# Six plain contraction tiles instead of two in each down projection, and the table of relative positions made in the mixer

## The chip, the cores and the metric

The kernel runs on one core of one Trainium2 chip. The metric is the device time of one execution in microseconds (us). TensorE (PE) multiplies, VectorE (DVE), ScalarE (ACT) and GpSimd (POOL) work on tiles in on-chip memory, and two engines issue the DMAs: SP the plain loads and stores, POOL those that add to their destination.

## The reference

A decoder layer on 512 tokens of width 1024, in float32: a half-step feed-forward block, a mixer of two kinds of attention, attention into a memory, a second feed-forward block; each is added to the residual stream and normalised. The parts that matter here:

```python
def swiglu(x, w1, w3, w2):
    return (jax.nn.silu(x @ w1) * (x @ w3)) @ w2          # D_FF = 2816 = 22 tiles of 128

h = layer_norm(ALPHA * h + 0.5 * swiglu(h, ffn1_w1, ffn1_w3, ffn1_w2), ln1_g, ln1_b)
mix = parallel_mixer(h, rel_bias, ...)                    # bias = rel_bias[t5_bucket(q_pos, k_pos)]
h = layer_norm(ALPHA * h + mix, ln2_g, ln2_b)
h = layer_norm(ALPHA * h + memory_attention(h, mem, ...), ln3_g, ln3_b)
h = layer_norm(ALPHA * h + 0.5 * swiglu(h, ffn2_w1, ffn2_w3, ffn2_w2), ln4_g, ln4_b)
```

`parallel_mixer` also needs one number `lam`, made from four short vectors by `exp(sum(q1*k1)) - exp(sum(q2*k2)) + lam_init`.

## The kernel before

Every float32 operand is split into a high and a low part (`split`: a cast, and a subtraction for the rest), and every product is three matmuls: high by high, high by low, low by high. A weight tile so split is called `..._hl`.

**Feed-forward block** (`ffn`, run as block 1 and block 4). The 22 contraction tiles f of the down projection are the 22 row tiles of the up projection. Tiles 0 and 1 of the up projection are plain. Tiles 2 to 21 come in ten pairs p1 to p10: `seven(p)` makes the 2x2 blocks of weights and tokens (or sums of them) meet in seven products instead of eight, each of 24 matmuls of 128x256, named `px`, `pz`, `py`, with weight blocks `wp_b` and their splits `wp_hl`. The down projection does the same for groups of four contraction tiles: `down7(g)` has seven products of 12 matmuls of 128x512, `dx`, `dy`, `dz`, with weights `wd_b`, `wd_hl` and token forms `A`. The loop runs p1, p2, group 0, p3, p4, group 1, and so on: two up pairs, one down group, five times. Groups 0 to 3 copy each product to a tile `st` (ScalarE) and POOL's DMA adds it into `acc` in DRAM. Within the last group the four token tiles of `acc` are loaded back into `res.acc` (`load_acc`, eight loads by SP, which must wait for the adding DMAs), and group 4's products are added into them by VectorE, 14 adds. At last `res.add` takes contraction tiles 20 and 21 as plain products (`res_w`, 48 matmuls of 128x512 for four token tiles and two halves of the columns), adds them and normalises token tile by token tile (`Norm`: `nmu`, `u`, `sq`, `ms`, `rs` on POOL, then `acc`). After blocks 1 to 3, TensorE transposes each normalised tile (`trh`, 8 transposes a tile), since the next stage wants it transposed in `hT`.

**Tables.** A generator `tables` waits until the planner's clock stands at 200 us; then it loads the constants, makes the table of relative positions (`bias_table`: load of `hot`, two small matmuls `rel`, a copy to `rows`, a store to `bias_dram`) and the number `lam` (`lam_calc`: load, product, sum, Exp). This falls into p7 of block 1.

**Mixer.** After block 1 come the first four gate tiles (`pw_gm`), the latents (`cq` and `ckv` for four token tiles each, transposed as `trc`), and the attention heads: `qr`, `vm`, `qn`, `kn` are a head's projections, `sm` its scores, `e` the exponentials, `trp_m` their transposes, `om` the weighed values; further gate tiles `pgm` are filler in between.

**Order.** Nothing is placed by hand. `Issue` is a planner in the program: generators yield work, TensorE's matmuls are issued as they come, each advancing the planner's clock by an estimate, and the other engines' operations wait in a list and are issued when their estimated start is due. So one generator that yields elsewhere can change the order of unrelated instructions near it. Each engine then works strictly in the order issued. There are three raw weight buffers (`wraw`), five split ones (`wsplit`), 20 general slots (`slot`) and eight PSUM banks.

Of the kernel before, what the change touches and what calls it, by code (L numbers as in the profile page):

```python
# [10 lines left out]
F32 = mybir.dt.float32  # L11
# [183 lines left out]
def layer(ctx: ExitStack, tc: tile.TileContext, a: dict, out: bass.AP):  # L195
# [421 lines left out]
    def plan_ffn(n, w1, w3, w2):  # L617
# [18 lines left out]
        for f in (20, 21):  # L636
            W.plan(f"w2_{n}_{f}", w2[f * P:(f + 1) * P])

    def ffn(n, src, ready=None):
        res = Residual(n, src)  # L640
        gT, sums, raw = {}, {}, {}
# [24 lines left out]
        def seven(p, late=()):  # L666
# [3 lines left out]
            def out(c, half, ps, sign):  # L670
# [3 lines left out]
                if half and p == 10:  # L674
# [46 lines left out]

        def down7(g, forms):
# [9 lines left out]
            def add(pss, h, c, sign, new=False):  # L732
                if g == 4:
                    for t in range(2):
                        dst = res.acc[2 * h + t][:, c * 512:c * 512 + 512]
                        dve.tensor_tensor(dst, dst, pss[t], op=ALU.add if sign > 0 else ALU.subtract)
                elif g == 0 and new:
# [4 lines left out]
                else:  # L742
                    st = slot(f"st{n}_{g}_{h}_{c}", F32)
                    for t in range(2):
                        act.activation(st[:, t], pss[t], AF.Copy, scale=sign)
                    pool.dma_start(rows(acc[h, c]), st, accum_op=ALU.add)
# [51 lines left out]
        for g in range(5):  # L798
            yield from seven(2 * g + 1)
            forms = Forms(g)  # L800
            late = {3: lambda: forms.make(1), 2: lambda: forms.make(2), 4: lambda: forms.make(5)}
            if g == 4:
                late[1] = load_acc
            yield from seven(2 * g + 2, late)
            yield from down7(g, forms)
        yield from res.add(lambda i, t: hl_of(gT[20 + i], slice(t * P, (t + 1) * P)), [f"w2_{n}_{f}" for f in (20, 21)], False, True)
# [4 lines left out]
    def bias_table():  # L811
# [4 lines left out]
        sp.dma_start(hot, a["onehot"])  # L816
        rows = arena.tile([8, REL], F32, tag="slot", name="rows")
# [5 lines left out]
        sp.dma_start(bias_dram.rearrange("h (p m) -> h p m", p=32), rows.unsqueeze(1).broadcast_to([8, 32, REL]))  # L823

# [4 lines left out]
    def lam_calc():  # L829
        room = slot("lam", F32, [P, 1024])  # L830
# [328 lines left out]
    def mixer():  # L1159
# [28 lines left out]
        ready = [h_ready[1, t] for t in range(NT)]  # L1188
        early = yield from project_halves([f"w_gm{j}" for j in range(EARLY)], ready)
# [219 lines left out]
    def tables():  # L1409
        mark = Mark()  # L1410
        mark.floor = 200000.0
        yield mark
        consts()
        bias_table()
        lam_calc()
# [100 lines left out]
```

## Time and profile before

| | |
|---|---|
| median of 3 runs | 1260.99 us (1260.83 to 1263.0) |
| profiled execution, its own time | 1261.45 us |
| its span | 1259.7 us |
| mean granted clock of TensorE | 0.988 |
| TensorE busy | 1214.5 us, 96%, 7530 matmuls |
| VectorE busy | 1019.4 us, 81%, 1590 instructions |
| ScalarE busy | 551.0 us, 44% |
| GpSimd busy | 105.5 us, 8% |

The times in the rows below are counted from the start of the span. A clock of 1.00 is 2.4 GHz, one of 0.50 is 1.2 GHz. A share of busy time says nothing of one stage; the rows are therefore cut to stages. In a timeline, "[4.41 <-DMA hot]" means that the engine stood idle 4.41 us just before and that the landing of `hot` ended it.

### The profile page before, as it was taken

To read this page: it belongs to the slowest core of one execution; us is meant where nothing else is said; L and a number is where in the kernel's file an instruction comes from. 1 tells how busy PE (TensorE), PEld (TensorE's weight loads), DVE (VectorE), ACT (ScalarE), POOL (GpSimd) and SP (SyncE) were. 2 spreads that over 40 slices of the span, in tenths; PEclk is the share of its full clock that TensorE was granted. 3 is DMA by queue.
4 is the path that set the end of the run, shared out by engine and by line. 5 is a ranking of instruction groups with operands and counts; after the bars stand their busy time and mean duration, and the time that the engine had idled before them with its cause. 6 is when DMAs were issued, how large, how long until landed. Compare 5 with 4: busy or idle time off the path is not lost. (4 is left out here: it accounts for less than half of the span.)

```text
span 1259.7 us, 19354 instructions
## 1 busy us (share of the span) xinstructions
PE 1214.5 (96%) x7530; PEld 1080.1 (86%) x7530; DVE 1019.4 (81%) x1590; ACT 551.0 (44%) x970; POOL 105.5 (8%) x101
## 2 busy tenths in 40 slices
PE   7999998999979999999999999999999999999995
PEld 5989897889869987877778889888899898999994
DVE  8999989789981799666665695555799999999998
ACT  5343635254432477434441244342453445445451
POOL 0001111111010000000000000000010102130300
PEclk9999999899979999999999999999999999999998
DMA  9749596869231321242233436244493667795941
GB/s 328 220 130 270 114 255 140 201 131 287 73 134 55 124 65 34 64 138 84 84 101 100 150 137 214 72 129 151 162 295 97 173 195 185 184 236 140 254 140 67
DMA packets 86591, 192.52 MB, mean 153 GB/s; under 512 B 7875, under 2 KB 9667, under 8 KB 86500
## 3 DMA queue, kind: packets, MB, share of 16 engines
q1 hardware_dynamic: 68004, 155.64, 37.1%
q0 software_dynamic: 18496, 35.66, 16.1%
q8 instruction: 59, 0.97, 0.3%
q14 instruction: 32, 0.26, 0.1%
HBM read 152.86 MB, written 38.40 MB: 152 GB/s over the span
## 5 line engine op out<-in xcount | busy, mean ns | idle before, releaser
L178 DVE TENSOR_TENSOR wp_hl<-wp_b,wp_hl 128x1024 fp32r<-128x1024 f32 x140 | 168.2, 1220 | 12.9 <-ACT wp_hl L178 10.6
L260 PE MATMUL pzwp<-S,wp_hl 128*128 128x256 f32 x960 | 124.2, 286 | 0.3 <-DVE S L178 0.3
L260 PE MATMUL pxwp<-S,wp_hl 128*128 128x256 f32 x960 | 122.6, 283 | 1.6 <-ACT p_wp L178 1.6
L260 PEld LDWEIGHTS pzwp<-S,wp_hl 128*128 128x128 f32 x960 | 120.0, 194 | 1.6 <-issue 1.1
L260 PE MATMUL pxwp<-hT,wp_hl 128*128 128x256 f32 x960 | 119.9, 281 | 1.3 <-ACT wp_hl L178 1.3
L260 PEld LDWEIGHTS pxwp<-hT,wp_hl 128*128 128x128 f32 x960 | 117.3, 188 | 4.2 <-ACT wp_hl L178 1.7
L260 PEld LDWEIGHTS pxwp<-S,wp_hl 128*128 128x128 f32 x960 | 118.3, 191 | 2.0 <-ACT p_wp L178 2.0
L178 ACT CAST wp_hl<-wp_b 128x1024 fp32r<-128x1024 f32 x75 | 78.7, 1051 | 93.3 <-PE pxwp L260 51.6
L260 PE MATMUL dx<-wd_hl,A 128*128 128x512 f32 x480 | 117.4, 391 | 1.6 <-DVE acc L178 1.2
L260 PEld LDWEIGHTS dx<-wd_hl,A 128*128 128x128 f32 x480 | 88.2, 188 | 21.2 <-issue 3.2
L178 DVE TENSOR_TENSOR wp_b<-wp_b,wp_b 128x1024 f32<-128x1024 f32 x80 | 97.4, 1219 | 0.6
L178 DVE TENSOR_TENSOR wd_hl<-wd_b,wd_hl 128x1024 fp32r<-128x1024 f32 x70 | 85.2, 1220 | 9.2 <-ACT wd_hl L178 9.2
L170 POOL DMA_DIRECT2D acc<-st x48 | 59.5, 1561 | 379.7 <-ACT st L178 205.1
L178 ACT CAST wd_hl<-wd_b 128x1024 fp32r<-128x1024 f32 x52 | 54.5, 1052 | 54.5 <-PE pxwp L260 24.9
L260 PE MATMUL pywp<-hT,wp_hl 128*128 128x256 f32 x480 | 60.6, 280 | 0.3 <-ACT wp_hl L178 0.3
L260 PE MATMUL dz<-wd_hl,A 128*128 128x512 f32 x240 | 59.2, 392 | 0.5 <-ACT st L178 0.3
L260 PEld LDWEIGHTS pywp<-hT,wp_hl 128*128 128x128 f32 x480 | 58.3, 188 | 0.5 <-ACT wp_hl L178 0.5
L260 PE MATMUL pw<-hT,w_hl 128*128 128x256 f32 (+1 forms) x288 | 49.8, 333 | 6.8 <-DVE w_hl L178 5.0
L260 PEld LDWEIGHTS dz<-wd_hl,A 128*128 128x128 f32 x240 | 44.5, 188 | 11.0 <-ACT st L178 1.1
L260 PEld LDWEIGHTS pw<-hT,w_hl 128*128 128x128 f32 x288 | 42.2, 194 | 13.5 <-ACT hT L178 7.2
L178 DVE CAST wp_hl<-wp_b 128x1024 fp32r<-128x1024 f32 x65 | 46.1, 710 | 7.4 <-PE pzwp L260 6.1
L260 PE MATMUL pgd<-hT,w_gd_hl 128*128 128x512 f32 x192 | 47.5, 400 | 0.0
(333 smaller groups left out, 2300.9 us busy)
## 6 DMA issues: line engine op xcount, KB each, us to landing
wp_b<-in_ffn_w SPq DMA_DIRECT2D x160, 256.0 KB, 6.9
wd_b<-in_ffn_w SPq DMA_DIRECT2D x50, 512.0 KB, 10.0
acc<-st POOLq DMA_DIRECT2D x48, 512.0 KB, 9.9
wd_b<-in_ffn_w POOLq DMA_DIRECT2D x20, 512.0 KB, 12.9
h_dram<-acc SPq DMA_DIRECT2D x12, 512.0 KB, 3.1
w_raw<-in_ffn_w SPq DMA_DIRECT2D x11, 512.0 KB, 5.3
w_gm_raw<-in_w_gate SPq DMA_DIRECT2D x8, 512.0 KB, 3.5
acc<-old SPq DMA_DIRECT2D x8, 512.0 KB, 3.7
```

Of the source, the lines that this page charges most:

```text
L170: return (name, 1000.0, 4000.0, lambda: getattr(engine, op)(*args, **kw)), args[:1], list(args)
L178: return (name, ns, 1500.0 if name == "sync" else 0.0, lambda: getattr(engine, op)(*args, **kw)), outs, ins
L260: issue.pe(lambda: nc.tensor.matmul(ps, w, x, start=start, stop=stop, skip_group_check=again), ps, w, x)
```

## The change

In both feed-forward blocks group 4 is no longer a seven-product group. After p9 a new generator `down` makes the plain products of contraction tiles 16 and 17 (48 matmuls `ds`), which go the way of groups 0 to 3: ScalarE copies them to `st` (`stage`), POOL adds them into `acc` by four DMAs. Then p10 follows, and `load_acc` is called ahead of its product 2. `res.add` takes four contraction tiles, 18 to 21, so 96 matmuls. The gated tiles 16 to 19 are split as they are finished; p10's results are split by halves of the tokens into `ends` (tiles `ge`). In all 144 matmuls of 128x512 stand for 84 + 48 = 132.

`bias_table` and `lam_calc` leave `tables`. They are spawned in the mixer when block 1's last tile is normalised, and between the load of `hot` and `rel` there is a planned delay of 15 us (`later`). `lam` gets its room from the pool `wk` instead of a slot.

```diff
-        for g in range(5):
+        for g in range(4):
             units += [up(2 * g + 1), up(2 * g + 2), down(g)]
+        units += [up(9), up(10)]
...
-                if half and p == 10:
+                if p == 10:
+                    if half not in ends:
+                        ends[half] = slot(f"ge{n}_{half}").rearrange("p c (i t) -> p c i t", i=2)
+                    split(ends[half][:, c, 0], ends[half][:, c, 1], dst)
+                elif half and p > 7:
                     f = 2 * p + c
                     gT[f] = slot(f"g{n}_{f}")
                     split(gT[f][:, 0], gT[f][:, 1], gated[:, c])
...
+        def stage(pss, h, c, sign):
+
+            st = slot(f"st{n}_{h}_{c}", F32)
+            for t in range(2):
+                act.activation(st[:, t], pss[t], AF.Copy, scale=sign)
+            pool.dma_start(rows(acc[h, c]), st, accum_op=ALU.add)
+
+        def down(fs):
+
+            keys = [f"w2_{n}_{f}" for f in fs]
+            ws = [W.take(key) for key in keys]
+            for h in range(2):
+                for c in range(2):
+                    pss = [bank(f"ds{n}_{h}_{c}_{t}") for t in range(2)]
+                    for t in range(2):
+                        for w, f in zip(ws, fs):
+                            toks = slice((2 * h + t) * P, (2 * h + t + 1) * P)
+                            mm3(pss[t], hl_of(gT[f], toks), hl_of(w, slice(c * 512, c * 512 + 512)), f == fs[0], f == fs[-1])
...
+                    stage(pss, h, c, 1.0)
+                    drop(*pss)
+                    yield
...
             def add(pss, h, c, sign, new=False):
-                if g == 4:
-                    for t in range(2):
-                        dst = res.acc[2 * h + t][:, c * 512:c * 512 + 512]
-                        dve.tensor_tensor(dst, dst, pss[t], op=ALU.add if sign > 0 else ALU.subtract)
-                elif g == 0 and new:
+                if g == 0 and new:
...
-        yield from res.add(lambda i, t: hl_of(gT[20 + i], slice(t * P, (t + 1) * P)), [f"w2_{n}_{f}" for f in (20, 21)], False, True)
+        yield from seven(9)
+        yield from down(range(16, 18))
+        yield from seven(10, {2: load_acc})
+        fs = range(18, NF)
...
+        yield from res.add(part, [f"w2_{n}_{f}" for f in fs], False, True)
...
         sp.dma_start(hot, a["onehot"])
+        yield later(15000.0)
...
+        lam_calc()
+        yield
...
-        room = slot("lam", F32, [P, 1024])
+        room = wk("lam")
...
+        issue.spawn(bias_table(), 8, ready[NT - 1])
...
         consts()
-        bias_table()
-        lam_calc()
```

Three places show how the instructions of TensorE move. A row is the line, the operation, output <- inputs, the shape and how many such matmuls stand in a row.

In p7 of block 1, before:

```order
L260 MATMUL pxwp_7_2232<-hT_89,wp_7_1_hl 128x256 x24
L260 MATMUL pxwp_7_2232<-S_1_119,wp_7_6_hl 128x256 x4
L260 MATMUL rel_2274<-hot,rel 8x320
L260 MATMUL rel_2278<-hot,rel 8x320
L260 MATMUL pzwp_7_2292<-S_0_118,wp_7_5_hl 128x256 x24
L260 MATMUL pxwp_7_2232<-S_1_119,wp_7_6_hl 128x256 x20
```

and now:

```order
L260 MATMUL pxwp_7_2232<-hT_89,wp_7_1_hl 128x256 x24
L260 MATMUL pzwp_7_2269<-S_0_118,wp_7_5_hl 128x256 x24
L260 MATMUL pxwp_7_2232<-S_1_119,wp_7_6_hl 128x256 x24
L260 MATMUL pzwp_7_2269<-S_0_118,wp_7_3_hl 128x256 x6
L260 MATMUL pzwp_7_2269<-S_1_119,wp_7_3_hl 128x256 x6
```

The `rel` matmuls are gone, and the products of p7 stand as in the other pairs. They now stand between the second and the third `cq` tile of the mixer.

At the end of block 1, before (`res_w` of the last token tile, then the transposes):

```order
L260 MATMUL res_w_1_20_3_0_3595<-w_1_21_hl,g_21_3282 128x512 x3
L260 MATMUL res_w_1_20_3_1_3604<-w_1_20_hl,g_20_3351 128x512 x3
L260 MATMUL res_w_1_20_3_1_3604<-w_1_21_hl,g_21_3282 128x512 x3
L269 MATMUL trh_0_0_3637<-ident,acc_0_3119 128x128 x4
L269 MATMUL trh_0_1_3642<-ident,acc_0_3119 128x128 x4
L269 MATMUL trh_1_0_3651<-ident,acc_1_3120 128x128 x4
L269 MATMUL trh_1_1_3657<-ident,acc_1_3120 128x128 x4
L269 MATMUL trh_2_0_3681<-ident,acc_2_3121 128x128 x4
L269 MATMUL trh_2_1_3686<-ident,acc_2_3121 128x128 x4
```

and now:

```order
L260 MATMUL res_w_1_18_1_1_3486<-w_1_21_hl,ge_0_3304 128x512 x3
L269 MATMUL trh_0_0_3508<-ident,acc_0_3345 128x128 x4
L269 MATMUL trh_0_1_3513<-ident,acc_0_3345 128x128 x4
L260 MATMUL res_w_1_18_2_0_3522<-w_1_18_hl,g_18_3095 128x512 x3
L260 MATMUL res_w_1_18_2_0_3522<-w_1_19_hl,g_19_3031 128x512 x3
L260 MATMUL res_w_1_18_2_0_3522<-w_1_20_hl,ge_1_3335 128x512 x3
L260 MATMUL res_w_1_18_2_0_3522<-w_1_21_hl,ge_1_3335 128x512 x3
L260 MATMUL res_w_1_18_2_1_3542<-w_1_18_hl,g_18_3095 128x512 x3
L260 MATMUL res_w_1_18_2_1_3542<-w_1_19_hl,g_19_3031 128x512 x3
L260 MATMUL res_w_1_18_2_1_3542<-w_1_20_hl,ge_1_3335 128x512 x3
L260 MATMUL res_w_1_18_2_1_3542<-w_1_21_hl,ge_1_3335 128x512 x3
L269 MATMUL trh_1_0_3564<-ident,acc_1_3346 128x128 x4
```

The transposes of a tile stand behind the products of the tile after it, where all came behind the last `res_w`; those of the last tile stand inside the first half of `pw_gm`.

In the first MLA head of the mixer, before:

```order
L260 MATMUL qn_4390<-cT_4116,w_qn_hl 128x512 x3
L260 MATMUL qn_4390<-cT_4122,w_qn_hl 128x512 x3
L260 MATMUL qn_4390<-cT_4129,w_qn_hl 128x512 x3
L260 MATMUL kn_4391<-cT_4291,w_kn_hl 128x512 x3
L260 MATMUL kn_4391<-cT_4298,w_kn_hl 128x512 x3
L260 MATMUL pgm_4323<-hT_89,w_gm_hl 128x512 x6
L260 MATMUL pgm_4323<-hT_90,w_gm_hl 128x512 x12
L260 MATMUL sm_3_4451<-kT_4276,qT_4407 128x512 x3
```

and now:

```order
L260 MATMUL pgm_4311<-hT_90,w_gm_hl 128x512 x4
L260 MATMUL qn_4378<-cT_4104,w_qn_hl 128x512 x2
L260 MATMUL kn_4379<-cT_4279,w_kn_hl 128x512 x3
L260 MATMUL kn_4379<-cT_4286,w_kn_hl 128x512 x3
L260 MATMUL pgm_4311<-hT_90,w_gm_hl 128x512
L260 MATMUL qn_4378<-cT_4104,w_qn_hl 128x512
L260 MATMUL qn_4378<-cT_4110,w_qn_hl 128x512 x3
L260 MATMUL qn_4378<-cT_4117,w_qn_hl 128x512 x3
L260 MATMUL pgm_4311<-hT_90,w_gm_hl 128x512 x7
L260 MATMUL sm_3_4439<-kT_4264,qT_4395 128x512
```

`kn` has come in ahead of the end of `qn`. Of the 18 gate matmuls `pgm` that stood behind `kn` before, 10 now stand ahead of `qn` (the last four of them are the first row), one within it and 7 behind. Further on the heads' order is the same.

## Rows read from the trace of the kernel before

**Rows 1.** Windows: length, busy PE, PEld, DVE, ACT, POOL (count), clock, DMA share, GB/s

```profile
1116.69:1175.75 59.06, 59.06 (x422) 55.75 (x422) 54.90 (x67) 28.98 (x46) 11.05 (x9) 1.00 0.79 196
152.96:212.03 59.07, 59.07 (x422) 55.75 (x421) 54.77 (x66) 28.87 (x46) 11.52 (x9) 1.00 0.80 195
212.03:283.94 71.91, 65.39 (x426) 57.85 (x424) 54.50 (x70) 30.09 (x47) 10.93 (x9) 0.93 0.78 176
283.94:394.74 110.80, 100.64 (x694) 93.45 (x692) 90.82 (x129) 41.84 (x62) 9.34 (x9) 0.94 0.50 148
```

**Rows 2.** Timeline of TensorE in round p7: start, us, what, [idle before, releaser]

```profile
221.81 2.30 PE L260 MATMUL rel<-hot,rel 33*8 33x320 f32 x4 [4.41 <-DMA hot<-in_onehot]
224.04 5.13 PE L260 MATMUL pzwp<-S,wp_hl 128*128 128x256 f32 x24
```

**Rows 3.** Window of 2 us inside round p7, columns as in rows 1

```profile
222.00:224.00 2.00, 2.00 (x4) 0.27 (x2) 0.97 (x3) 0.20 (x1) 2.00 (x2) 0.50 0.93 96
```

**Rows 4.** Timeline of SP, which issues the loads, round p7

```profile
215.51 0.37 SPq L178 DMA_DIRECT2D hot<-in_onehot  x1
```

**Rows 5.** Timeline of TensorE, end of the first feed-forward block

```profile
359.23 3.68 PE L269 MATMUL trh<-ident,acc 128*128 128x128 f32 x16 [3.33 <-DVE acc L178]
368.89 3.48 PE L269 MATMUL trh<-ident,acc 128*128 128x128 f32 x16 [5.98 <-DVE acc L178]
372.13 22.77 PE L260 MATMUL pw_gm<-hT,w_gm_hl 128*128 128x256 f32 x192
```

**Rows 6.** Window of 2 us at that end

```profile
360.00:362.00 2.00, 2.00 (x11) 2.00 (x10) 2.00 (x8) 1.17 (x2) 0.00 (x0) 0.50 1.01 399
```

**Rows 7.** Timeline of TensorE in the w_o stage

```profile
735.79 1.03 PE L269 MATMUL trh<-ident,acc 128*128 128x128 f32 x8
736.58 5.72 PE L260 MATMUL res_w_o<-w_o_hl,zT 128*128 128x512 f32 x24
742.14 1.03 PE L269 MATMUL trh<-ident,acc 128*128 128x128 f32 x8
```

**Rows 8.** Timeline of TensorE, end of the second feed-forward block

```profile
1235.46 2.88 PE L260 MATMUL dx<-wd_hl,A 128*128 128x512 f32 x12
1238.18 9.23 PE L260 MATMUL res_w<-w_hl,g 128*128 128x512 f32 x40
```

**Rows 9.** Timeline of VectorE: w_o stage (first three), end of the program

```profile
731.02 0.68 DVE L178 SCALAR_TENSOR_TENSOR acc<-acc,res_w_o 128x512 f32<-128x512 f32 x1
...
734.15 1.28 DVE L178 SCALAR_TENSOR_TENSOR acc<-u,rs_ln,lnb 128x1024 f32<-128x1024 f32 x1
...
742.34 0.69 DVE L178 SCALAR_TENSOR_TENSOR acc<-acc,res_w_o 128x512 f32<-128x512 f32 x1 [0.36 <-PE res_w_o L260]
...
1255.22 1.42 DVE L178 SCALAR_TENSOR_TENSOR acc<-u,rs_ln,lnb 128x512 f32<-128x512 f32 x2 [0.73 <-POOL rs_ln L178]
```

**Rows 10.** DMA issues, 1176 to 1262: queue, count, KB each, median us to landing

```profile
acc<-acc SPq DMA_DIRECT2D x8, 256.0 KB, 8.3
...
acc<-st POOLq DMA_DIRECT2D x3, 512.0 KB, 12.1
```

**Rows 11.** Timeline of TensorE, first MLA head

```profile
454.09 1.25 PE L269 MATMUL trp_m<-ident,e 128*128 128x128 f32 x10
```

**Rows 12.** Timeline of VectorE, first MLA head

```profile
442.51 0.69 DVE L178 TENSOR_SCALAR qT<-qn 64x512 fp32r<-64x512 f32 x1
...
448.78 0.69 DVE L178 CUSTOM_DVE_ANT_0 e<-sm,mask 128x512 f32<-128x512 f32 x1
```

**Rows 13.** Groups of TensorE, 425 to 520: busy, mean ns, idle before and releasers

```profile
L269 PE MATMUL trp_m<-ident,e 128*128 128x128 f32 x75 | 10.2, 273 | 2.0 <-DVE e L178 1.2 <-DVE kT L178 0.7
```

**Rows 14.** All DMAs of tile `acc`, 1176 to 1262

```profile
DMA to landing us min/median/max: 2.0/8.0/14.9
```

**Rows 15.** DMA issues, 284 to 375, columns as in rows 10

```profile
acc<-acc SPq DMA_DIRECT2D x8, 256.0 KB, 11.5
```

**Rows 16.** Waits of SP, 1116 to 1200: us in all, times, longest

```profile
SPq L178 <- DMA acc<-st: 49.9, 10, 13.2
```

More of the change, by code (lines that the diff above doesn't have):

```diff
@@ L635, in plan_ffn @@
             u.plan()
-        for f in (20, 21):
+            if u is units[-2]:
+                for f in (16, 17):
+                    W.plan(f"w2_{n}_{f}", w2[f * P:(f + 1) * P])
+        for f in range(18, 22):
             W.plan(f"w2_{n}_{f}", w2[f * P:(f + 1) * P])
@@ L640, in ffn @@
         res = Residual(n, src)
-        gT, sums, raw = {}, {}, {}
+        gT, ends, sums, raw = {}, {}, {}, {}
         acc = {(h, c): dram.tile([256, 512], F32, name=f"acc{n}_{h}_{c}") for h in range(2) for c in range(2)}
@@ L720, in load_old @@
                     sp.dma_start(t, rows(src[256 * h:256 * h + 256, c * 512:c * 512 + 512]))
+        def stage(pss, h, c, sign):
[13 more added lines that the diff above has]
+                            mm3(pss[t], hl_of(gT[f], toks), hl_of(w, slice(c * 512, c * 512 + 512)), f == fs[0], f == fs[-1])
+                    if h and c:
+                        for key in keys:
+                            W.done(key)
+                    stage(pss, h, c, 1.0)
+                    drop(*pss)
+                    yield
         def down7(g, forms):
@@ L742, in add @@
                 else:
[L743 to L746, printed above, removed]
+                    stage(pss, h, c, sign)
             x = [bank(f"dx{n}_{g}_{t}") for t in range(2)]
@@ L797, in ffn, with part @@
         load_old()
-        for g in range(5):
+        for g in range(4):
             yield from seven(2 * g + 1)
             forms = Forms(g)
[L801 to L804, printed above, removed]
+            yield from seven(2 * g + 2, {3: lambda: forms.make(1), 2: lambda: forms.make(2), 4: lambda: forms.make(5)})
             yield from down7(g, forms)
-        yield from res.add(lambda i, t: hl_of(gT[20 + i], slice(t * P, (t + 1) * P)), [f"w2_{n}_{f}" for f in (20, 21)], False, True)
+        yield from seven(9)
+        yield from down(range(16, 18))
+        yield from seven(10, {2: load_acc})
+        fs = range(18, NF)
+        def part(i, t):
+            if i < 2:
+                return hl_of(gT[fs[i]], slice(t * P, (t + 1) * P))
+            return [ends[t // 2][:, i - 2, j, t % 2 * P:t % 2 * P + P] for j in (0, 1)]
+        yield from res.add(part, [f"w2_{n}_{f}" for f in fs], False, True)
     bias_dram = dram.tile([8, 32 * REL], F32, name="bias_dram")
@@ L823, in bias_table, with later @@
         sp.dma_start(bias_dram.rearrange("h (p m) -> h p m", p=32), rows.unsqueeze(1).broadcast_to([8, 32, REL]))
+        lam_calc()
+        yield
+    def later(ns):
+        mark = Mark()
+        mark.floor = issue.clock + ns
+        return mark
     neglam = const.tile([P, 1], F32, name="neglam")
@@ L1409, in tables @@
     def tables():
-        mark = Mark()
-        mark.floor = 200000.0
-        yield mark
+        yield later(200000.0)
         consts()
-        bias_table()
-        lam_calc()
     def main():
```

## The prediction

> **What bounds the kernel now.** I read the engines' shares first (TensorE 96% busy, VectorE 81%), then windows cut at the borders of whole stages, then TensorE's timeline inside the windows that were too long. The windows say where time can be had. One full round of a feed-forward block (two up projections of seven products, one down group) takes 59.06 us with TensorE busy throughout at clock 1.00 and VectorE busy 54.90 [rows 1]; a round of the first block takes 59.07. Nothing can be got there but by fewer matmuls. Two windows of the first block are out of line [rows 1]: the round that begins with product tile p7 takes 71.91 us at clock 0.93, and the stretch from p9 to the mixer's `cq` takes 110.80 us, of which TensorE works 100.64 at clock 0.94.
>
> The timeline gives the reason for each. In p7 TensorE stands 4.41 us for the load of `hot`, then does the four `rel` records in 2.30 us and a product of 24 in 5.13 us [rows 2], at a granted clock of 0.50, that is 1.2 GHz [rows 3]. The load was late because SP issued it only at 215.51 [rows 4], 3.5 us into the round. At the end of the block TensorE finishes its matmuls, then waits 3.33 and 5.98 us for VectorE's `acc` before two batches of transposes `trh` [rows 5]; VectorE is busy 2.00 of 2.00 us there, and the clock is at 0.50 [rows 6]. So at the end VectorE is the bound: it adds the seven products of group 4 into `res.acc` one by one and then has four tiles to normalise.
>
> **The change part by part.** One 128x512 matmul costs 0.2267 us: 12 of them lie between 1235.46 and 1238.18 [rows 8], 2.72 us. A seven-product down group has 84, 19.04 us; two up projections have therefore 59.06 - 19.04 = 40.02 us [rows 1].
>
> *A, the table leaves p7.* `hot`, the two `rel` products and the `lam` loads go away, and with them the wait, the half-clock stretch and two activation-table loads on ScalarE. On every engine the p7 round is then the same as its neighbours, so it costs what they cost: 71.91 - 59.06 = **-12.85 us**. From this round on VectorE also splits two gated tiles in place of later work, about 2 us of a margin of 59.06 - 54.90 = 4.2 [rows 1]; I cost it at nothing, and if that cover failed the price would be those 2 us.
>
> *B, the end of the first block.* Group 4 had 84 matmuls and the plain pair 48; now there are 48 (`ds`) and 96 (`res`): 12 more, 2.72 us. In return no product of group 4 is added by VectorE (14 adds), seven weight splits become four, and the sums of the A forms vanish; `res` runs at four keys, 2.72 us per half tile, so VectorE gets 5.44 us for each token tile, and the chain of one tile from the first add to the last normalising step is 734.15 - 731.02 = 3.13 us plus 1.28 [rows 9]. The new order puts the transposes of a tile one tile later, among matmuls, just as the w_o stage has them; there 8 transposes take 736.58 - 735.79 = 0.79 us without a wait [rows 7]. The last tile's transposes stand behind most of the first half of `pw_gm`. So the window is 40.02 + 48 x 0.2267 + 96 x 0.2267 + 4 x 0.79 + `pw_gm` 22.61 (372.13 to 394.74 [rows 5]) = 98.4 us. I add 0.7 for the last split of `ge`, which depends on p10's last product and is wanted 8 matmuls (1.8 us) later, and for VectorE's first tile. 110.80 - 99.1 = **-11.7 us**. Ends: none of the waits returns (98.4) or both do in full, which is a rival below.
>
> *C, the mixer.* `rel` now stands between two `cq` tiles, and SP asks for `hot` ahead of three `cq` weights that are needed before it, so I cost no wait: half of 2.30 us, at full clock, 1.15 [rows 2, 3]. SP has `lam` behind one `w_gm` load and `bias_dram` ahead of the next; the rows have nothing waiting on either. The planner's other order in the first MLA head is the larger term. Ahead of the end of `qn` 11 gate matmuls and 6 of `kn` are slipped in, 17 x 0.2267 = 3.9 us. VectorE begins on `qT` when `qn` is done and reaches the first `e` 448.78 - 442.51 = 6.3 us later [rows 12] with hardly a gap, so `e` and the transposes that TensorE wants from it slip by up to 3.9 us; some of VectorE's other work can go ahead in the gap. TensorE has only 2.0 us of waits on these transposes in the whole stretch [rows 13], so it would feel it. Bounds 0 and 3.9; I take 2.5, nearer to the upper end since VectorE is full there. Sum C **+3.6 us**.
>
> *D, the end of the second block.* Same counts, no transposes: p9 begins at 1175.75, so TensorE ends at 1175.75 + 40.02 + 10.88 + 21.76 + 0.5 (the `ge` split) = 1248.9. In the kernel before it ends near 1238.18 + 9.23 = 1247.4 [rows 8], but VectorE is behind and begins its last normalising step only at 1255.22 [rows 9]. After the last matmul the chain costs 0.2 (from TensorE's next work at 742.14 [rows 7] to 742.34 [rows 9] in the w_o stage), 3.13, and from 1255.22 to the end of the span 4.48: 1256.7. Against 1259.7: **-3.0 us**.
>
> Sum: -12.85 - 11.7 + 3.6 - 3.0 = -23.9. The profiled execution took 1261.45 (span 1259.7, 1.75 around it): 1237.5. It lies 0.46 above the median 1260.99, so **1237 us**.
>
> **The rivals.** *1. The first head's other order is hidden*, because VectorE uses the gap: C is 1.15, the time 1234.5. For it: work that doesn't need `qn` stands in the queue. Against: it is in order, with `qT` ahead of `kT`. Chance 0.15.
>
> *2. The accumulated sums come late.* The four `ds` results go to DRAM by accumulating DMAs, and the eight loads of `acc` must wait for these. The loads land in 8.3 us (median, second block), the accumulates in 12.1 [rows 10], the slowest access of `acc` in 14.9 [rows 14]; the first block's loads took 11.5 [rows 15]. By the new order SP issues the loads about 11 us into p10 in the second block and 13.7 in the first (behind a `w_gm` load which waits for a buffer), and VectorE wants them 20.0 + 2.7 = 22.7 into it: 11.7 and 9.0 us of time. Medians fit or nearly so (11.5 against 9.0); at 14.9 both are late, by 3.2 and 5.9, and the time is 1237 + 9.1 = 1246. For it: the chain of accumulate, wait, load is closer to its use than before, when VectorE added group 4 in SBUF. Against: no weight blocks of a group 4 are loaded beside it, so the queues are emptier. The Trainium skill bears on this chance ("DMA: Bandwidth & Descriptors", section "Two DMAs through the same engine are not ordered"): a DMA that reads what another wrote has to wait for the other's semaphore, so the two latencies add and neither hides the other. The trace agrees as far as SP stood 49.9 us for `acc<-st` in ten waits [rows 16]. Chance 0.13; middle 1243.
>
> *3. The stall only moves to the mixer*: `rel` waits for `hot` between two `cq` tiles and the clock falls as in p7. The price is what p7 paid beyond the work itself, 12.85 - 1.15 = 11.7 at most: 1249. Against: the planned delay of 15 us, and the place of `hot` in SP's order. Chance 0.05.
>
> *4. VectorE is not what the ends wait for*: if the chain of adds, sums and normalising were as long with fewer adds, only A and C would remain, and the 24 more matmuls would cost 5.4: 1261 - 12.85 + 3.6 + 5.4 = 1257, near no change. Against: [rows 6]. Chance 0.04.
>
> *5. Slower*, by rival 2's mechanism carried further: loads so late at both ends that TensorE runs dry and its clock drops to 0.50 again. It decides from 13 us of loss at each end, that is loads that land some 24 us after issue; the slowest shown is 14.9. Beyond that point the time is 1237 + 26 = 1263 and more. Chance 0.03.
>
> **How the numbers follow.** Forecast 0.60, rivals 0.15, 0.13, 0.05, 0.04, 0.03. The forecast's own spread, from C's ends and from 0 to 2.5 us more at the first block's end, is 1234 to 1240. Rival 1 reaches to 1232.5, if the `ge` split costs nothing either; rival 2 to 1246. Range **1232.5 to 1246**, which leaves out rivals 3 to 5 and a little of both ends. A measurement tells some 0.2% (2.5 us) from no change. Faster by more: 0.60 + 0.15 + 0.13 + 0.05 and a part of rival 4, 0.94; within 0.03; slower 0.03.
>
> **What would show it.** The p7 round at 59.1 us with clock 1.00 (A). From p9 to `cq` 99 us, with no wait of TensorE over 1 us before `trh` (B); a wait there for `acc` released by a DMA would be rival 2, by VectorE rival 4. `rel` 1.2 us without a wait; the first `trp_m` some 2.5 us later after `cq` than before, 454.09 - 394.74 = 59.4 us [rows 1, 11], plus `rel` (C). The last matmul 7.8 us before the end of the span (D). It would be wrong if the p7 round kept a wait that the rows put down to `hot` but which has another cause, or if the reordered first head cost more than 4 us.

## The result and the profile after

| | before | after |
|---|---|---|
| median, same chip | 1261.74 us (1260.83 to 1263.0) | 1241.32 us (1240.77 to 1243.1) |
| span of the profiled execution | 1259.7 us | 1241.3 us |
| mean granted clock of TensorE | 0.988 | 0.996 |

The ratio is 0.984, with a 95% interval of 0.9823 to 0.9857: 1.6% faster, 20.4 us less. The forecast was 1237 us, 24 us less, with a range of 1232.5 to 1246. So direction and range held, and the forecast was 4.3 us too low. The profiled execution of after is the slowest of its four (1243.1 us); the same kernel was therefore run and profiled once more beside the last experiments (`c1_after_again`).

To see where the time went, I cut the span of each kernel at five instructions of TensorE: the first of p7, of p9, of `cq`, of the first MLA head's `qr` (four such heads follow one another from there), and of `vd`, the projection that begins the next part of the mixer. In us:

| kernel | median | p7 to p9 | p9 to `cq` | `cq` to `qr` | `qr` to `vd` | `vd` to end |
|---|---|---|---|---|---|---|
| before | 1261.7 | 71.91 | 110.80 | 39.77 | 68.01 | 757.13 |
| after | 1241.3 | 59.07 | 99.12 | 40.71 | 75.74 | 754.38 |
| after, again | 1242.6 | 59.07 | 100.16 | 40.70 | 73.43 | 754.59 |

The two long windows of [rows 1] are gone. Windows of after, round p7 and p9 to `cq` (length, busy PE, PEld, DVE, ACT, POOL with counts, clock, DMA share, GB/s):

```profile
212.31:271.39 59.08, 59.08 (x422) 55.77 (x421) 55.58 (x70) 27.66 (x44) 11.07 (x9) 1.00 0.82 202
271.39:370.50 99.11, 99.11 (x705) 93.05 (x704) 76.65 (x112) 34.21 (x54) 12.43 (x11) 1.00 0.64 170
```

TensorE is busy in all of both and its clock is 1.00; VectorE, at the end of the block the bound before, has 22 us to spare in 99. The timeline of TensorE shows `trh` without a wait where [rows 5] had 3.33 and 5.98 us, and `rel` between two `cq` tiles without one where [rows 2] had 4.41 us:

```profile
333.39 1.03 PE L269 MATMUL trh<-ident,acc 128*128 128x128 f32 x8
...
356.81 1.04 PE L269 MATMUL trh<-ident,acc 128*128 128x128 f32 x8
...
379.07 1.24 PE L260 MATMUL rel<-hot,rel 33*8 33x320 f32 x4
```

The end of the program, TensorE's last matmuls and then VectorE's last normalising, which answers to [rows 8, 9]:

```profile
1232.03 1.52 PE L260 MATMUL res_w<-w_hl,ge 128*128 128x512 f32 x6
```

```profile
1233.59 0.69 DVE L178 SCALAR_TENSOR_TENSOR acc<-acc,res_w 128x512 f32<-128x512 f32 x1 [0.23 <-PE res_w L260]
...
1236.77 1.42 DVE L178 SCALAR_TENSOR_TENSOR acc<-u,rs_ln,lnb 128x512 f32<-128x512 f32 x2 [0.73 <-POOL rs_ln L178]
```

From TensorE's last matmul (1233.55) to the end of the span (1241.33) are 7.78 us; VectorE takes up the last sum 0.2 us after its matmul and no longer lags.

What was lost lies in the mixer, from `cq` to `vd`: 107.78 us before, 116.45 after, 114.13 in its second profile. Windows `cq` to `qr` and `qr` to `vd`, of before, of after, and of after again:

```profile
394.74:434.51 39.77, 39.54 (x249) 37.85 (x247) 18.57 (x33) 14.91 (x38) 5.09 (x8) 1.00 0.31 101
434.51:502.52 68.01, 65.17 (x373) 55.10 (x371) 65.39 (x171) 49.15 (x115) 0.00 (x0) 1.00 0.19 57
```

```profile
370.50:411.21 40.71, 40.71 (x253) 37.99 (x251) 14.11 (x28) 15.95 (x40) 5.08 (x8) 1.00 0.38 90
411.21:486.95 75.74, 70.42 (x373) 57.12 (x373) 71.49 (x180) 48.44 (x115) 0.00 (x0) 0.95 0.21 66
```

```profile
371.18:411.88 40.70, 40.70 (x253) 37.97 (x251) 14.09 (x28) 15.97 (x40) 5.08 (x8) 1.00 0.38 90
411.88:485.31 73.43, 67.99 (x374) 54.38 (x373) 71.35 (x180) 48.25 (x115) 0.00 (x0) 1.00 0.21 68
```

After the length stand the engines' busy times, each with a count; VectorE's is the third of them. It did 18.57 us of work from `cq` to `qr` before and does 14.1 now, and 71.4 instead of 65.39 us afterwards, where it was full already. What it put off are splits of weights (`w_gm`, `w_kn`, `w_v`) and steps that come behind them. The loads of these weights are late. The DMA issues of after from 371 to 412 and, below, those of before from 395 to 435 (KB each, median us from issue to landing; of the three `w_gm` loads of after the trace tells the landing of the second alone, issued at 387.58):

```profile
w_gm_raw<-in_w_gate SPq DMA_DIRECT2D x3, 512.0 KB, 10.6
bias_dram<-rows SPq DMA_DIRECT2D x1, 640.0 KB
w_kn_raw<-in_w_kn SPq DMA_DIRECT2D x1, 512.0 KB, 10.9
...
w_qr_raw<-in_w_qr SPq DMA_DIRECT2D x1, 192.0 KB, 7.2
```

```profile
w_gm_raw<-in_w_gate SPq DMA_DIRECT2D x3, 512.0 KB, 3.5
w_kn_raw<-in_w_kn SPq DMA_DIRECT2D x1, 512.0 KB, 4.5
...
w_qr_raw<-in_w_qr SPq DMA_DIRECT2D x2, 192.0 KB, 3.4
```

The transfers that are new in after are `lam`, 128 KB, which landed at 377.8, before the slow loads were issued, and the table's store to `bias_dram`, 640 KB, issued at 380.86. While the store is alone in flight the window reads:

```profile
383.00:387.00 4.00, 4.00 (x24) 4.00 (x24) 1.27 (x3) 1.05 (x3) 0.86 (x1) 1.00 0.49 51
```

DMA engines 0.49 busy, yet only 51 GB/s moved. The store's source is eight partitions, and the Trainium skill ("DMA: Bandwidth & Descriptors", section "Rules for kernel authors") says that an outermost dimension below 16 confines a DMA to at most so many of the 16 engines; the share of 0.49, just under 8 of 16, agrees.

The late landing is not, however, what VectorE waits for in after. It works strictly in the order issued, and the planner gave it another order. The split of the second `w_gm` tile in before, then VectorE's timeline in after with the same split as the third row:

```profile
414.04 0.71 DVE L178 CAST w_gm_hl<-w_gm_raw 128x1024 fp32r<-128x1024 f32 x1 [0.53 <-DMA w_gm_raw<-in_w_gate]
```

```profile
400.46 0.15 DVE L178 TENSOR_SCALAR ms_ckv<-ssq_ckv 128x1 f32<-128x1 f32 x1 [3.02 <-ACT sq_ckv L178]
403.64 0.15 DVE L178 TENSOR_SCALAR ms_ckv<-ssq_ckv 128x1 f32<-128x1 f32 x1 [3.03 <-ACT sq_ckv L178]
403.71 0.68 DVE L178 CAST w_gm_hl<-w_gm_raw 128x1024 fp32r<-128x1024 f32 x1
...
425.53 0.69 DVE L178 TENSOR_SCALAR qT<-qn 64x512 fp32r<-64x512 f32 x1
...
433.00 0.69 DVE L178 CUSTOM_DVE_ANT_0 e<-sm,mask 128x512 f32<-128x512 f32 x1 [0.54 <-PE sm L260]
```

In before the split stands ahead of the first `ms_ckv`, 19.3 us after `cq`, and waits 0.53 us for its load. In after it stands behind the last `ms_ckv`, 33.2 us after `cq`. Its load (387.58, 10.6 us) had landed at 398.2; VectorE stood still for ScalarE's `sq_ckv` in the meantime, and no wait for this load shows. So in after the changed order already puts the split off; what the late load costs where VectorE does wait for it is seen in e11 below.

`qT` begins 14.3 us after `qr`'s start (411.21) and the first `e` 21.8; before it was 8.0 and 14.3 [rows 12, counted from 434.51 in the window above]. TensorE pays with the longest wait of the four heads, before the first scores:

```profile
427.52 4.16 PE L260 MATMUL sm<-kT,qT 96*128 96x512 f32 x14 [1.94 <-ACT qT L178]
```

### The profile page after: what moved, and what is told of

It reads as the page before. It is cut to its first block, busy times and chain, and to the rows that moved or that the text cites. A ratio compares the mean times of both kernels' runs of the same rounds, so it can differ in the third digit from the quotient of the medians.

```text
span 1241.3 us, 19337 instructions
## 1 busy us (share of the span) xinstructions
PE 1216.4 (98%) x7554; PEld 1083.7 (87%) x7554; DVE 996.3 (80%) x1565; ACT 533.5 (43%) x953; POOL 111.3 (9%) x105
## 4 chain that ended last, share of the span: by engine, by line
PE 87%; DVE 8%; ACT 2%; issue 1%; DMA 1%; SPq 0%; POOL 0%; DVEq 0%; POOLq 0%; ACTq 0%
PE pxwp L260 18%; PE pzwp L260 9%; PE dx L260 7%; PE pywp L260 4%; PE mq L260 4%; PE res_w_o L260 4%; PE res_w L260 3%; PE pgd L260 3%; PE res_mem_w_o L260 3%; PE dz L260 3%; PE pw L260 2%; PE mk L260 2%; PE vd L260 2%; PE pw_gm L260 2%; PE qd L260 2%; PE kd L260 2%
## 5 line engine op out<-in xcount | busy, mean ns | idle before, releaser
L170 POOL DMA_DIRECT2D acc<-st x56 | 69.5, 1561 | 425.8 <-ACT st L178 229.1
L178 ACT CAST wp_hl<-wp_b 128x1024 fp32r<-128x1024 f32 x69 | 72.1, 1052 | 78.4 <-PE pxwp L260 42.2
L260 PE MATMUL dx<-wd_hl,A 128*128 128x512 f32 x384 | 93.1, 390 | 0.4 <-DVE old L178 0.4
L260 PEld LDWEIGHTS dx<-wd_hl,A 128*128 128x128 f32 x384 | 70.7, 188 | 14.8 <-issue 1.1
L178 DVE TENSOR_TENSOR wd_hl<-wd_b,wd_hl 128x1024 fp32r<-128x1024 f32 x56 | 68.4, 1221 | 9.0 <-ACT wd_hl L178 8.9
L178 ACT CAST wd_hl<-wd_b 128x1024 fp32r<-128x1024 f32 x42 | 44.2, 1052 | 43.7 <-PE pxwp L260 22.2
L178 DVE CAST wp_hl<-wp_b 128x1024 fp32r<-128x1024 f32 x71 | 50.0, 704 | 8.9 <-PE ds L260 3.9
L260 PE MATMUL dz<-wd_hl,A 128*128 128x512 f32 x192 | 46.7, 390 | 0.0
L260 PE MATMUL mq<-hT,mem_wq_hl 128*128 128x512 f32 x192 | 46.1, 398 | 0.0
## 6 DMA issues: line engine op xcount, KB each, us to landing
wd_b<-in_ffn_w POOLq DMA_DIRECT2D x16, 512.0 KB, 14.3
```

Source lines behind the costliest of these rows:

```text
L170: return (name, 1000.0, 4000.0, lambda: getattr(engine, op)(*args, **kw)), args[:1], list(args)
L178: return (name, ns, 1500.0 if name == "sync" else 0.0, lambda: getattr(engine, op)(*args, **kw)), outs, ins
L260: issue.pe(lambda: nc.tensor.matmul(ps, w, x, start=start, stop=stop, skip_group_check=again), ps, w, x)
```

## The experiments

Theory: each of the prediction's four terms, A (the table out of p7), B and D (the ends of the two blocks), C (the mixer), is what its part of the change does, and C is what the table costs where it now lies. Rivals are named at each run. All runs are timed against before on the same chip, whose medians there were 1261.72 to 1262.25.

### The two parts of the change apart

`e1_table_to_mixer` is the kernel before with the second part of the change alone:

```diff
         sp.dma_start(hot, a["onehot"])
+        yield later(15000.0)
...
+        lam_calc()
...
+        issue.spawn(bias_table(), 8, ready[NT - 1])
...
-        bias_table()
-        lam_calc()
```

> The kernel before with the table alone moved to the mixer. Terms A and C without B and D. Its first MLA head keeps vm, qn, kn and 18 gate matmuls in the order of before; only the passes of sm are interleaved. Theory (the 8.9 us that the changed kernel lost between cq and vd come from kn and gate matmuls ahead of the end of qn, and from the clock that falls in the wait that follows): the p7 round takes 59.1 us, cq to vd 108 to 110, the time is 1261.7 - 12.85 + 1.2 = 1250. Rival (the table's own work in the mixer costs it, its loads, rel, lam's Exp and the table load of ScalarE): cq to vd 115 or more, 1257 to 1258.

1253.83 us, ratio 0.9939 (0.9922 to 0.9955). p7 to p9 took 59.07, as in after; p9 to `cq` kept its length (111.55); `cq` to `vd` took 111.99, 4.2 more than before, though the feed-forward blocks are the old ones. So the table alone is worth 12.8 us in p7 and costs about 4 in the mixer. The time lies between the theory's and the rival's.

`e2_ffn_only` is after with `bias_table()` and `lam_calc()` back in `tables`, without a delay:

```diff
-        issue.spawn(bias_table(), 8, ready[NT - 1])
...
         consts()
+        bias_table()
+        lam_calc()
```

> The changed feed-forward blocks with the table left in p7. Terms B and D alone. Theory (the terms add up): the p7 round takes 71.9 us again, p9 to cq 99.1, cq to vd 107.8 as before, since the planner's order of the first head is that of before; 1241.3 + 12.85 - 8.7 = 1245.5. Rival (the block's end gained because the round ahead of it no longer stalls): p9 to cq well over 101 us, and a time of 1249 or more.

1241.47 us, ratio 0.9839 (0.9823 to 0.9856), as fast as after itself. p9 to `cq` took 98.92 and the end 754.24: B and D belong to the new ends alone. `cq` to `vd` took 107.82, as before: C comes only with the table in the mixer. But p7 to p9 took 66.63, not 71.9. The planner had put `rel` behind four products of p7 where one stood ahead of it before (and four matmuls of another), `hot` was there in time, and 7.6 us were lost all the same. Hence the next two runs.

The two parts of the change don't add up. Beside before on the same chip e1 is 8.1 us faster, e2 20.4, and both together are 20.4 faster too. With the new ends the planner's other order already takes 5.3 us out of p7, so moving the table gains 7.6 there and loses 6.3 to 8.6 in the mixer (the two profiles of after): beside the new ends it buys nothing.

### What the table costs in p7

`e3_table_p7_delay` is after with the table in p7, but `hot` and `lam` loaded 15 us (planner's time) ahead of their use:

```diff
+        room = lam_load()
         yield later(15000.0)
...
-        issue.spawn(bias_table(), 8, ready[NT - 1])
...
         consts()
+        yield from bias_table()
```

> The changed kernel, but the table stays in the first feed-forward block, with the planned delay of 15 us between its loads (hot and lam) and its use. Theory: the stall was only the short distance of load and use, so rel goes through in p8 in 1.2 us, and the first head has the order of before: 1241.3 - 8.7 = 1232.6 (rel is in either). Rival (loads land much later than 15 us there, where 16 weight blocks are in flight, or ScalarE's two table switches hold up p8): 1238 to 1245.

1245.18 us, ratio 0.9866 (0.9852 to 0.9881): the rival's value. The mixer was as before (108.04), p7 to p9 took 68.36. VectorE's timeline in e3 has the reason:

```profile
221.85 0.29 DVE L178 TENSOR_TENSOR lam<-lam 128x128 f32<-128x128 f32 x1 [3.79 <-DMA lam<-in_lam]
```

In its strict order it waits 3.79 us for the 128 KB of `lam`, which is most of the 4.2 us by which a round leaves it idle. TensorE then waits for it all through the round, at last in the down group:

```profile
232.44 5.31 PE L260 MATMUL pxwp<-hT,wp_hl 128*128 128x256 f32 x42 [1.61 <-DVE p_wp L178]
...
263.10 4.14 PE L260 MATMUL dy<-wd_hl,A 128*128 128x512 f32 x10 [1.67 <-DVE A L178]
```

e2 has the same wait of VectorE, 4.05 us at 221.18.

`e4_before_delay` is the kernel before with the delay after the load of `hot` and nothing else:

```diff
         sp.dma_start(hot, a["onehot"])
+        mark = Mark()
+        mark.floor = issue.clock + 15000.0
+        yield mark
```

> The kernel before with one edit: 15 us of planned delay between the load of hot and its use. lam is still loaded and used at once. Theory (TensorE stood for hot alone): p7 and the rounds after it lose no more than rel, 1261.7 - 12.85 + 1.2 = 1250. Rival (lam's wait on VectorE and ScalarE holds up TensorE too): a stall of up to 6 us and a clock drop remain, 1254 to 1260.

1255.71 us, ratio 0.9948 (0.9933 to 0.9963): the rival's value, but not its mechanism, since VectorE has no wait for `lam` here. p7 to p9 took 64.02: the delay takes 7.9 of the 12.85 us out, and leaves `rel` (1.24 us) and waits for VectorE and ScalarE such as this, of TensorE:

```profile
258.67 0.73 PE L260 MATMUL dy<-wd_hl,A 128*128 128x512 f32 x2 [1.70 <-ACT A L178]
```

So the wait for `hot` with its half clock was the larger part of the long round. What makes up the other 5 us was not taken apart: in e2 and e3 VectorE's wait for `lam` stands in the round, in e4 it doesn't, and the order of instructions differs too. In every kernel that keeps the table or its loads in the block the round is longer than 59.07.

### The ends of the blocks

`e7_dve_adds` is after with two more VectorE adds of 128x512 into an unused tile at each of the seven products of p10, 14 a block, as many as group 4 had:

```diff
-        yield from seven(10, {2: load_acc})
+        yield from seven(10, {1: burden(2), 5: burden(2), 6: burden(2), 3: burden(2), 7: burden(2), 2: burden(2, load_acc), 4: burden(2)})
```

> The changed kernel with 14 more adds of 128x512 on VectorE (14 x 0.68 = 9.5 us) during p10 in each feed-forward block, as many as group 4 had; their result is not used. VectorE has 99.1 - 76.7 = 22.5 us free from p9 to cq. Theory B (VectorE was the bound at the end and now has room): the first block's end takes 0 to 3 us more, the second 0 to 2, 1241 to 1246. Rival (the adds themselves were the whole of the 12 us): 9 us more in the first block and 3 in the second, 1253.

1243.98 us, ratio 0.9856 (0.9841 to 0.9871). p9 to `cq` took 100.76, which is 1.6 and 0.6 more than in the two profiles of after; the second block's part kept its length (754.26). At 0.68 us each, the adds are some 9.6 us of VectorE's time at each end. The planner gave four casts to ScalarE for them, so VectorE's busy time from p9 to `cq` rose by 6.0 us (76.65 to 82.60), and of that little shows. VectorE is no longer the bound there.

`e8_load_late` calls `load_acc` one product later (the products run in the order 1, 5, 6, 3, 7, 2, 4):

```diff
-        yield from seven(10, {2: load_acc})
+        yield from seven(10, {4: load_acc})
```

> The changed kernel with the loads of acc called one product later (2.9 us). It measures the slack of the loads. Main theory (they land with time to spare): no change, 1241 within 1. Rival 2 (they land just in time): up to 2.9 us more in each block, 1244 to 1247, with a wait of VectorE for acc.

1245.35 us, ratio 0.9867 (0.9847 to 0.9887). p9 to `cq` took 102.48, 2.3 to 3.4 more; the second block lost nothing. TensorE of e8, then VectorE:

```profile
336.81 1.09 PE L269 MATMUL trh<-ident,acc 128*128 128x128 f32 x8 [2.65 <-DVE acc L178]
```

```profile
329.08 0.69 DVE L178 SCALAR_TENSOR_TENSOR acc<-acc,res_w 128x512 f32<-128x512 f32 x1 [1.49 <-DMA acc<-acc]
...
333.66 1.28 DVE L178 SCALAR_TENSOR_TENSOR u<-acc,nmu,lng 128x1024 f32<-128x1024 f32 x1 [1.42 <-DMA lng<-in_ln_g]
```

In the first block SP issued the eight loads at 323.07, where after has 316.87 (its timeline): two more `w_gm` loads had gone ahead of them, so the move was 6.2 us and not the 2.9 of a product. The sums then came 1.49 us late and `lng`, loaded behind them, 1.42 more. Rival 2 did not happen in after, but with 6.2 - 1.49 - 1.42 to 6.2 - 1.49, some 3 to 5 us in hand in block 1, it was near.

### The mixer: what the table costs there

`e5_delay5` is after with a shorter planned delay, 5 us instead of 15, so that the store comes sooner:

```diff
-        yield later(15000.0)
+        yield later(5000.0)
```

> The changed kernel with one number altered: the planned delay of the table in the mixer is 5 us instead of 15. The table's work in the mixer is the same, rel stands in the second half of pw_gm. The planner's first head has vm, qn, kn, 18 gate matmuls in the order of before. Theory (the head's order and the clock cost the 8.9 us): cq to vd 108 to 110, no wait of TensorE ahead of sm, 1241.3 - 7.5 = 1234. Rival (the table's own work costs it): no change, 1241.

1240.15 us, ratio 0.9827 (0.9812 to 0.9842). The four heads took 69.63, without the wait in the first, but the latents now had one (41.89), on TensorE:

```profile
409.92 0.33 PE L269 MATMUL trc<-ident,cn 128*128 128x128 f32 x1 [2.18 <-ACT cn L178]
```

In sum 111.52, 2.6 less than in the second profile of after; the time is near the rival's value, and the gain of the heads went into the latents.

e5 also shows how the store slows a load. The store was issued at 367.24; one `w_gm` load, issued at 373.98, landed 10.4 us later. Windows while the load's first half moves, while nothing of it moves, and while its second half does:

```profile
376.00:378.50 2.50, 2.50 (x16) 2.50 (x15) 0.15 (x1) 1.16 (x3) 0.55 (x1) 1.00 0.80 154
378.50:381.80 3.30, 3.30 (x21) 3.30 (x20) 0.15 (x1) 0.58 (x2) 0.55 (x1) 1.00 0.46 51
382.00:384.40 2.40, 2.40 (x15) 2.40 (x14) 0.00 (x0) 0.39 (x1) 0.00 (x0) 1.00 0.40 161
```

By the trace's packets 64 of the load's 128 start between 376.4 and 378.1, at 159 ns each as in before, and the other 64 only from 382.4; the last packet of the store ends at 382.1. So half of the load goes at full pace, and the half on the store's DMA engines waits until the store is through. A load of `w_ckv`, issued at 370.64, shows the same two halves.

`e6_fill_gap` puts eight matmuls of no use (their bank is overwritten) where TensorE waits 1.94 us in the first head, to hold the clock:

```diff
+                if h == 0 and i == NT - 1:
+                    for j in range(8):
+                        matmul(sc, wkn[:, 0, :P], ckvT[0][:, 0], True, True)
```

> The changed kernel with 8 matmuls of 128x512 (8 x 0.227 = 1.8 us) into sm's own bank ahead of the first score product, whose results are overwritten by it: they take up most of TensorE's wait of 1.94 us and nothing else. Theory (most of the loss is the clock at 0.50 after that wait): sm begins at the same time as before, the clock stays at 1.00, and cq to vd shrinks by 3 to 5 us: 1237 to 1238. Rival (the loss is VectorE's lateness, the clock is by the way): cq to vd unchanged, 1241.

1243.93 us, ratio 0.9862 (0.9841 to 0.9882). The clock stayed at 1.00 through the place, and `qr` to `vd` still took 75.90: the wait came back behind it, where TensorE needs what VectorE makes of the transposes.

```profile
447.62 0.44 PE L260 MATMUL om<-ptm,vm 128*64 128x512 f32 x1 [2.47 <-DVE ptm L178]
```

So a clock that holds does not by itself shorten this stretch; VectorE is busy 22.77 of the 24 us from 426 to 450. It is not a clean test of the clock, since the planner counts the eight matmuls too and the order behind them is another.

`e10_loads_early` leaves the table in the mixer but loads `hot` and `lam` in p7, into one slot, and makes the table as soon as it is spawned:

```diff
+    def table_loads():
+        rel = table["rel"] = const.tile([33, 8], F32, name="rel")
...
+        room = table["hot"] = slot("hot", F32, [P, 1024])
+        sp.dma_start(room[:33, :REL], a["onehot"])
+        sp.dma_start(room[:, 640:896], a["lam"].partition_broadcast(P))
...
         consts()
+        table_loads()
```

> The changed kernel with the loads of hot and lam in the first block and the arithmetic (rel, rows, lam) in the mixer, in pw_gm. Its first head has the order of before. Theory (the loads and the store of the table, between the weight loads of SP, shifted VectorE's weight splits into the heads): cq to vd 108 to 109, p9 to cq 100.3, 1235. Rival (VectorE's own 1.6 us of the table in the mixer cost it): cq to vd 110 or more, 1238 to 1241.

1249.5 us, ratio 0.99 (0.9885 to 0.9915), far off both. `cq` to `vd` took 114.10 without any load of the table in it, so C does not need these loads. The store, sooner now, met other loads: the three of `w_ckv_raw` landed after 12.3, 10.2 and 8.1 us, and TensorE waited 3.02 us in `ckv` for its split. The rest of the loss is in p7 to p9, 66.48, where I had only added the two loads. ScalarE's timeline there, in e10 and, below, in after again:

```profile
274.14 0.60 ACT L178 ACTIVATE st<-dx 128x512 f32<-128x512 f32 x1 [6.50 <-DMA acc<-st]
```

```profile
273.20 1.09 ACT L178 ACTIVATE st<-dx 128x512 f32<-128x512 f32 x2 [4.03 <-DMA acc<-st]
```

ScalarE waits for a slot that an adding DMA still reads, longer in e10, and TensorE stood 5.07 us for it. `hot` held one of the 20 slots from p7 into the mixer, and I take it that the round lacked it; that was not tried by itself.

`e9_table_in_p9` loads both in p7 in the same way, makes the table some 50 us later, and spawns nothing in the mixer:

```diff
-        issue.spawn(bias_table(), 8, ready[NT - 1])
...
+        table_loads()
+        yield later(50000.0)
+        yield from bias_table()
```

> The changed kernel with the table in p9 of the first block, where VectorE has 22 us free up to cq, its loads issued 50 us of planned time earlier, and lam's arithmetic placed after rel, so that no engine waits for a load. Theory (the table costs only its 1.2 us on TensorE where VectorE has room; the mixer without it has its order of before): p7 round 59.1, p9 to cq 100.3, cq to vd 107.8, 1241.3 - 7.5 = 1234. Rival (two table switches of ScalarE and lam hold up any stretch of the block): p9 to cq over 104, 1238 or more.

1242.04 us, ratio 0.9843 (0.9829 to 0.9858). The mixer was as before (107.77) and there was no wait for `hot` or `lam`, but p7 to p9 took 64.06 by the same wait for `st`, and p9 to `cq` 101.55. The time is the rival's, though the loss lies elsewhere than it said. TensorE:

```profile
271.92 4.36 PE L260 MATMUL dx<-wd_hl,A 128*128 128x512 f32 x12 [3.39 <-ACT st L178]
```

`e11_store_pool` is after with the store issued by POOL instead of SP:

```diff
-        sp.dma_start(bias_dram.rearrange("h (p m) -> h p m", p=32), rows.unsqueeze(1).broadcast_to([8, 32, REL]))
+        pool.dma_start(bias_dram.rearrange("h (p m) -> h p m", p=32), rows.unsqueeze(1).broadcast_to([8, 32, REL]))
```

> The changed kernel with one word altered: the store of bias_dram is issued by POOL, not by SP, where it stood ahead of the weight loads and waited for rows. Loads, rel and lam stay where they are, and TensorE's first head has the order of before. Theory (the store in SP's queue is what changed the order): cq to vd 109, 1241.3 - 7.5 = 1234. Rival (lam's load and wait did): cq to vd 112 or more, 1238 to 1241.

1240.61 us, ratio 0.9832 (0.9816 to 0.9849). The sum, 112.80, and the time are the rival's values. The four heads came back to 68.69, but `cq` to `qr` took 44.11. VectorE's order is that of before again, with the second `w_gm` split ahead of the first `ms_ckv`. The load is still slow beside the store (10.0 us), and now VectorE waits for it; ScalarE's `cn` waits behind VectorE, and TensorE for that. VectorE, then TensorE:

```profile
398.62 0.69 DVE L178 CAST w_gm_hl<-w_gm_raw 128x1024 fp32r<-128x1024 f32 x1 [7.14 <-DMA w_gm_raw<-in_w_gate]
```

```profile
402.01 0.66 PE L269 MATMUL trc<-ident,cn 128*128 128x128 f32 x4 [1.70 <-ACT cn L178]
```

The Trainium skill ("DMA: Bandwidth & Descriptors", section "Issuing engines are not separate DMA queues") says that DMAs of all issuing engines share the same 16 DMA engines; this run agrees: with another issuer the same load is as late (10.0 us against 10.6). What the issuer changed is the planner's order, and with it who waits.

`c1_after_again` is after, unchanged:

> The changed kernel itself, beside the three others on the same chip, so that they can be set against it: 1241, cq to vd 116.5, and the clock in the first head's stretch 0.95 to 1.00, as the runs with the same order have shown.

1242.55 us, ratio 0.9847 (0.9832 to 0.9862). The order of work and the wait of 1.94 us in the first head are the same as in after's first profile, and `qr` to `vd` is 2.3 us shorter. The difference that the rows show is the granted clock behind the wait; windows of after, then of after again:

```profile
430.23:434.23 4.00, 4.00 (x14) 3.52 (x13) 3.37 (x9) 0.50 (x1) 0.00 (x0) 0.50 0.19 40
```

```profile
431.00:435.00 4.00, 4.00 (x21) 3.28 (x20) 3.90 (x12) 1.10 (x3) 0.00 (x0) 1.00 0.15 42
```

So of the 7.73 us that this stretch grew in the first profile at most 2.3 are the clock (0.50 is 1.2 GHz), and 5.4 are there with the clock at 1.00 too.

In all, `cq` to `vd` over the kernels:

| the table is made | kernels | `cq` to `vd` |
|---|---|---|
| before the mixer | before, e2, e3, e4, e9 | 107.8, 107.8, 108.0, 108.1, 107.8 |
| in the mixer | e1, e5, e11, e10 | 112.0, 111.5, 112.8, 114.1 |
| in the mixer, as in after | after again, after, e6, e7, e8 | 114.1, 116.5, 116.6, 115.2, 114.1 |

The kernels of the second row have TensorE's first head in the order of before. In these the four heads take 68.67 to 69.63, and the loss lies in the latents (41.89 to 45.38 against 39.77). So the table costs time with either order of the first head; what goes with the order is where it shows.

## Why the prediction was right, and where it was off

The time lies inside the stated range, but above the forecast's own spread of 1234 to 1240. The upper part of the range had been added for rival 2, which did not happen; that it covered a loss in the mixer is luck.

**A was right, to 0.01 us** (-12.84 against -12.85): the round costs what its neighbours cost. The sum was taken from a neighbour and so didn't need the cause. The cause it named, the late `hot` and the half clock, is some 7.9 us of it (e4); with `hot` in time and `lam` still in the round 7.6 and 9.3 are lost (e2, e3).

**B was right**: -11.68, in the second profile -10.64, against -11.7. Its steps hold one by one: no wait before `trh`, VectorE with room (e7), the 12 more matmuls paid for by two waits and the half clock. That none of the `acc` loads would be late (rival 2) was right in block 1 with some 3 to 5 us in hand (e8). The prediction had set 9.0 us of time against a median landing of 11.5 there; in after the loads land after 5.1 (median). It also read [rows 16] for more than they hold: of those ten waits of SP for `acc<-st` only the last two, 14.0 of 49.9 us, stand ahead of loads of `acc`, and the other eight hold up loads of weights. Rival 4 is refuted by the result; rivals 3 and 5 didn't occur.

**D was right**: -2.75, second profile -2.54, against -3.0, by the chain that it named (7.78 us behind the last matmul, forecast 7.8).

**C is the term that was mis-sized**: +3.6 forecast, +8.67 measured in the first profile and +6.35 in the second. That the loss falls into the first head, where VectorE is full, was named rightly: from its `qr` to the next head's it takes 46.15 and, in the second profile, 43.81 us, against 37.62 before. That is 8.5 and 6.2 more, over the 4 us by which the prediction itself said it would be wrong. The kernels with and without the table in the mixer show that the table is the cause; but those with the first head of before lose 3.7 to 6.3 us as well, so the head's order is not all of it. Two sentences failed.
- "SP has `lam` behind one `w_gm` load and `bias_dram` ahead of the next; the rows have nothing waiting on either." I asked who waits for the store; what it does to the loads behind it, and to the order of VectorE, I didn't cost. The second `w_gm` load landed after 10.6 instead of 3.5 us, its split stands 33.2 instead of 19.3 us behind `cq`, and the work went into the stretch where VectorE is full. In e11, with VectorE's order of before, the late load alone makes VectorE wait 7.14 us. (`lam` is waited for as well, 2.11 us of VectorE at 377.82, where it had room.)
- "Bounds 0 and 3.9", taken from the 17 matmuls ahead of the end of `qn`. The order of TensorE's instructions gave that figure; but VectorE's `qT` came 6.3 us later after `qr` (14.3 against 8.0) and `e` 7.5 later, since VectorE had put-off work in front of it. A delay on a full engine is not bounded by what another engine slips in. What could have been read: VectorE had 68.01 - 65.39 = 2.6 us of room, and what is pushed into the stretch beyond that finds no cover.

The first profile's sum is 0.28 (up to p7) - 12.84 - 11.68 + 0.94 + 7.73 - 2.75 = -18.3 of the span, the second's -19.8; forecast -23.9. Of the 5.6 and 4.1 us between, C has 5.1 and 2.8, and B none and 1.1.

What stays open is how C divides between the late load and VectorE's changed order: e11 has the late load with the order of before, but no run has the order of after without the store. No run changed the store's shape either: spread over more partitions, or issued by ScalarE's queue, it wasn't tried. If C cost its `rel` alone (1.2 us), the time would be some 1237 us, an estimate: 1242.55 - (6.35 - 1.2), from after again. None of the versions that ran is clearly faster than after: e5 lies 1.2 us below its first median, e11 0.7 below that and 1.9 below after again on the same chip, with ratios whose intervals overlap.

## What to carry to other kernels

Cost a stage that is out of line by a neighbour of the same work, then ask what else besides the named wait must go before it is like its neighbour. When work is moved, cost its DMAs against the loads that will be in flight beside them, above all those into the stretch where an in-order engine is full: nobody needs to wait for a store for it to cost time. Compare the order of VectorE's instructions too, and not TensorE's alone. And what such an engine can absorb is its idle time in that stretch, 2.6 us here, 4.2 in a round.

## What the hardware showed that I had not expected

- A store of 640 KB from eight partitions made loads of 512 KB beside it land after 10.0 to 10.9 us (after, e5, e11), against 3.5 to 4.5 in before. It moved some 51 GB/s at a DMA share of 0.49, where a stretch of before with loads alone had 101 GB/s at 0.31. Half of a load's packets went through at once; the other half waited for the store's end (e5).
- The same wait of TensorE, 1.94 us at the same instruction, was followed by a granted clock of 0.50 in after, by 0.59 over the window below in e7, and by 1.00 in after again and in e8:

```profile
431.00:435.00 4.00, 4.00 (x15) 3.47 (x15) 3.61 (x6) 0.00 (x0) 0.00 (x0) 0.59 0.00 0
```

```profile
434.00:438.00 4.00, 4.00 (x21) 3.24 (x20) 3.91 (x12) 1.27 (x4) 0.00 (x0) 1.00 0.19 53
```

The first is e7, the second e8. So a wait of this length does not by itself decide the clock, and 2 us of a single profile's stretch can be the clock's alone.
